# A third FFN chunk by seven products, an even mixing rate, and every fourth plain FFN residual summed by an accumulating DMA

## The chip, the cores and the metric

The kernel runs on one core of one Trainium2 chip, as one program. The metric is the device time of one execution in microseconds; three runs are given, and one further execution was profiled.

## The reference, cut to what matters

Two layers, each a mixer and a SwiGLU feed-forward part (FFN), each followed by a layer norm, on x of 256 tokens by 2048, all in float32. The change lies in the FFN of both layers (D_FF is 5632, eleven chunks of 512):

```python
def swiglu(x, w_gate, w_up, w_down):
    return (jax.nn.silu(x @ w_gate) * (x @ w_up)) @ w_down
...
        y = swiglu(x, ffn_w_gate[layer], ffn_w_up[layer], ffn_w_down[layer])
        x = layer_norm(DEEPNORM_ALPHA * x + y, ln_g[layer, 1], ln_b[layer, 1])
```

## The kernel before, in words

**Precision by halves.** A float32 product is made of three matmuls: every operand w is split into a high half (a rounded copy, `wh`) and a residual (`wl` = w - wh). ScalarE writes the copy (L425) and VectorE the residual (L427). The activations are kept split as XH, XL (input of the FFN) and YH, YL (its gated product).

**Pieces and visits.** A chunk is 512 columns of one weight matrix; its name is its kind, layer and number (g0_2 is gate 2 of layer 0, u is up, d is down). A piece is 256 rows of a chunk (512 KB): gate and up chunks have 8, down chunks 4 or 6. A visit is the work of TensorE on one piece. A plain visit has 12 matmuls of 512 columns (L117 to L119). Gate chunks 2 to 10, and the up chunks in `UPS` (4 and 8), are done instead with seven products for eight, after Strassen: 21 matmuls of 256 columns a visit (L453 to L455). For that VectorE first makes combinations of the weights in the raw buffer (L383, L385, L386), ScalarE copies seven quarters (L389) and VectorE takes their residual (L392). When such a chunk is complete it is drained from its four PSUM banks (`drain_s`, one operation of ScalarE and five of VectorE), and an up chunk drained so is multiplied by the gate on VectorE (L1093). A plain up chunk is multiplied straight from PSUM (L1089, two operations). The combinations of the activations (XS) are made in four batches by `xs_batch` on VectorE and ScalarE (L901 to L914) during up 0.

**The order on TensorE** is written out beforehand in the list `visits`. `ffn_part` lists the plain visits (`flat`: gate 1, the plain ups, the downs of finished groups), and mixes the seven-product visits (`gates`) in: behind plain visit k of `flat` the amount `want` grows by a rate, and as many of them are placed as its whole part says. Behind the ends of odd ups (`near`) at least one is placed. `after_up` fixes the visits behind which the gated product of a chunk is transposed on TensorE (L602, by `h_T`) and split into YH and YL.

**Feeding.** The weights come through SP's queue (L360) into raw buffers: four for plain pieces (N), two for seven-product pieces (S); so too for the split results. In the stretch of a layer in which seven-product visits are mixed in, plain pieces may use N buffers only (`classes`). After every visit `feed_more` issues what loads and splits the free buffers allow, in order of the pieces; a split may run ahead of its visit by as many pieces as there are buffers. The loads are issued in order, and a load whose buffer is not free holds up all behind it. `feed_split` issues a split. For a seven-product piece the copy and the residual are kept back (`owe`), and issued with the next split (`pay`) or one visit later. Each engine works in the order of issue.

Of the kernel before, what the change touches and what calls it, by code (L numbers as in the profile page):

```python
# [9 lines left out]
F32 = mybir.dt.float32  # L10
F32R = mybir.dt.float32r
AF = mybir.ActivationFunctionType
ALU = mybir.AluOpType
# [40 lines left out]
def trunk_kernel(ctx: ExitStack, tc: tile.TileContext, x, ab_w_in, b_f, ab_w_out,  # L54
                 rel_bias, mla_w_in, q_g, kv_g, w_uq, w_ukv, mla_w_out, w_gate, w_up,
                 w_down, ln_g, ln_b, cst, out):
    nc = tc.nc
# [111 lines left out]
    for g in range(4):  # L169
        q0, k0, v0 = ((QA, KA, VA) if g < 2 else (QB, KB, VB))  # L170
        h4 = HB4[g] % 8
        if g == 0:
            c = add_chunk("v0", "X", K16, ([260, 260], lambda h: rows(
                w0, h * 256, [(0, 520, VA + 512)])), ("mm", "att"))
        else:
            c = add_chunk(f"v{g}", "X", K16, ([512], lambda h, a=v0 + h4 * P: rows(
                w0, h * 256, [(0, 512, a)])))
        kmajor(c)
        for u in range(2):
            a = (h4 + 2 * u) * P  # L180
            c = add_chunk(f"qk{g}{u}", "X", K16, ([512], lambda h, a=a, q0=q0, k0=k0: rows(
                w0, h * 256, [(0, 256, q0 + a), (256, 256, k0 + a)])))
# [14 lines left out]

    GROUPS = ((0, 1), (2, 3), (4, 5), (6, 7), (8, 9, 10))
    NF = 11
    UPS = (4, 8)  # L200
    PLAIN = (0, 1)
    h_done = set()
    after_up = {}
# [2 lines left out]
    def ffn_part(layer):  # L206
        def wide(nm, w, f):
            return add_chunk(f"{nm}{layer}_{f}", "X", K16, ([512], lambda h: rows(
                w[layer], h * 256, [(0, 512, f * 512)])))

        def down(gi):
            grp = GROUPS[gi]
            slots = [4 * (f % 4) + k for f in grp for k in range(4)]
            for n in range(4):
                c = add_chunk(f"d{layer}_{gi}_{n}", "Y", slots, (
                    [512], lambda h, n=n: rows(
                        w_down[layer], grp[0] * 512 + h * 256, [(0, 512, n * 512)])))
                if gi == len(GROUPS) - 1 and n == 3:
                    (lead_final if layer == 1 else lead_end)(c)
                else:  # L220
                    kmajor(c)

        g0 = wide("g", w_gate, 0)
        g0.pair = 0
        lead_begin(g0)
        base = len(visits)
        for f in range(NF):
            if f == 1:
                kmajor(wide("g", w_gate, 1))
            c = wide("u", w_up, f)  # L230
            if f in UPS:
                c.S = True
            else:
                kmajor(c)
            if f in (1, 3, 5, 7):
                down(f // 2)
        down(len(GROUPS) - 1)
        flat = visits[base:]
        del visits[base:]
        ends = {}  # L240
        for f in range(NF):
            if f not in UPS:
                e = ends[f] = max(k for k, v in enumerate(flat) if v[0].name == f"u{layer}_{f}")
                o = e + 2 - f % 2
                after_up[layer, f] = [(v[0].name, v[1], v[2]) for v in flat[o:o + 3]]
        gates = []
        for f in range(len(PLAIN), NF):
            c = wide("g", w_gate, f)
            c.S = True
            gates += [(c, h, (0, 1)) for h in range(8)]  # L250
            if f in UPS:
                gates += [(chunks[f"u{layer}_{f}"], h, (0, 1)) for h in range(8)]
        near = {ends[f] + 2 for f in (1, 3, 5, 7, 9)}
        ns, want = 0, 0.0
        for k, v in enumerate(flat):
            visits.append(v)
            want = max(want + (0 if k < 9 else 0.575 if k < 62 else 0.74 if k < 132 else 0.9),
                       ns + 1 if k in near else 0)
            while ns < min(len(gates), int(want)):
                visits.append(gates[ns])  # L260
                ns += 1
                c = gates[ns - 1][0]
                f = int(c.name[3:])
                if ns % 8 == 0 and c.name[0] == "g" and f not in UPS:
                    assert k < ends[f] - 1, (k, ns, ends)
        assert ns == len(gates)
        for f in UPS:
            e = max(k for k, v in enumerate(visits) if v[0].name == f"u{layer}_{f}")
            rest = [v for v in visits[e + 1:] if not v[0].S]
            o = next(k for k, v in enumerate(rest) if v[1] == 0)  # L270
            after_up[layer, f] = [(v[0].name, v[1], v[2]) for v in rest[o:o + 2]]
# [4 lines left out]
    c = add_chunk("m0", "X", K16, ([512], lambda h: rows(wi, h * 256, [(0, 512, 0)])))  # L276
    lead_begin(c)
    for i in (1, 2):
        c = add_chunk(f"m{i}", "X", K16, ([288], lambda h, i=i: rows(
            wi, h * 256, [(0, 288, 512 + 288 * (i - 1))])), ("att",) if i == 1 else None)  # L280
# [4 lines left out]
    for nm in order:  # L285
        p = int(nm[2:])
        if nm[0] == "u":
            c = add_chunk(nm, "X", [0, 1, 2, 3], ([384], lambda h, p=p: rows(
                w_uq[0], h * 256, [(0, 384, p * 384)])))
        else:  # L290
            c = add_chunk(nm, "X", [4, 5, 6, 7], ([512], lambda h, p=p: rows(
                w_ukv[0], h * 256, [(0, 512, p * 512)])))
# [6 lines left out]
    pieces = []  # L299
# [9 lines left out]
    first_s, last_s = {}, {}  # L309
# [4 lines left out]
    raw_free = [("N", feed.tile([P, HPMAX], F32, name=f"raw{i}")) for i in range(NR)]  # L314
# [5 lines left out]
    slot_of, rslot_of = {}, {}  # L320
# [44 lines left out]
    whole = {}  # L365
    owed = []
# [12 lines left out]
    def split_s(j):  # L379
# [14 lines left out]
        wts[j] = (sh.rearrange("p (q c) -> p q c", c=256), sl.rearrange("p (q c) -> p q c", c=256))  # L394
        return hi, lo

    def feed_split(j, halves=False, part=None):
        if j >= len(pieces):
            return False
        c, h = pieces[j]  # L400
        n = 2 * c.n
        if part != 1:
            got = take(w_free, j) if j in raws else None
            if got is None:
                return False
            slot_of[j] = got
            if c.S:
                new = split_s(j)
                for o in owed:
                    o["age"] += 1  # L410
                pay("act")
                pay("dve")
                owe(j, *new)
                return True
            r = raws.pop(j)
            wh, wl = got[1]
            wts[j] = (wh[:, :n].rearrange("p (k c) -> p k c", k=2),
                      wl[:, :n].rearrange("p (k c) -> p k c", k=2))
            whole[j] = (r, wh, wl)
        r, wh, wl = whole[j]  # L420
        cuts = [(0, c.n), (c.n, n)] if halves or part is not None else [(0, n)]
        if part is not None:
            cuts = [cuts[part]]
        for a, b in cuts:
            nc.scalar.activation(wh[:, a:b], r[:, a:b], AF.Copy)  # L425
            pay("act")
            nc.vector.tensor_tensor(wl[:, a:b], r[:, a:b], wh[:, a:b].bitcast(F32),  # L427
                                    op=ALU.subtract)
            pay("dve")
        if part != 0:  # L430
            whole.pop(j)
            raw_free.append(rslot_of.pop(j))
        for o in owed:
            o["age"] += 1
        return True
# [921 lines left out]
    for i, (c, h, toks, *half) in enumerate(visits):  # L1357
# [21 lines left out]
        if last_use[c.name, h] == i:  # L1379
            j = pid[c.name, h]  # L1380
# [81 lines left out]
```

## Time and profile before

| | us |
|---|---|
| median of three runs | 2145.41 |
| lowest and highest | 2145.27, 2146.47 |
| the profiled execution | 2146.55 |
| its span, first to last instruction | 2144.7 |
| TensorE busy in the span | 2120.4 |
| VectorE busy | 1674.0 |
| ScalarE busy | 1061.6 |
| GpSimd busy | 94.5 |

Matmuls are pipelined and the profile models their ends, so a busy TensorE is read by the starts of its instructions. The mixed stretch runs from about 463 to 1052 us in layer 0 and from about 1460 to 2050 in layer 1.

### The profile page before, as it was taken

The page shows a single profiled execution, that of the slowest core. Times are in us where ns is not written, and L with a number is a line of the kernel's source. Part 1 is how long each engine was busy: PE and PEld are TensorE (multiplying, and loading weights), DVE is VectorE, ACT ScalarE, POOL GpSimd, SP SyncE. Part 2 cuts the span into 40 slices and gives each one's busy share as a digit, 9 for nine tenths or more (in the row PEclk, how much of TensorE's full clock was granted, in tenths as well). Part 3 has the DMA queues.
Part 4 walks back from the last instruction along what each step waited for, and adds up shares of the span by engine and source line. Part 5 has one row for each costly group of instructions (what it writes and reads, how often), then busy time and mean ns, then how long its engine had stood idle before and what let it go on. Part 6 is the DMA issues. An engine that isn't in the chain of part 4 may idle for free.

```text
span 2144.7 us, 31708 instructions
## 1 busy us (share of the span) xinstructions
PE 2120.4 (99%) x12570; PEld 1864.7 (87%) x12570; DVE 1674.0 (78%) x2173; ACT 1061.6 (50%) x1212; POOL 94.5 (4%) x142
## 2 busy tenths in 40 slices
PE   9999999999999999999999999999999999999998
PEld 9899998788888888888888999878888888888886
DVE  5555656798888998899866676688888989889875
ACT  5444544355545555555534665445444555555551
POOL 2100000100000000000001331010000000000000
PEclk9999999999999999999999999999999999999999
DMA  8565555556555556555865533745555556555582
GB/s 287 176 204 165 172 184 199 198 174 207 195 191 190 189 190 203 187 187 184 295 193 164 176 129 137 284 139 182 188 189 192 180 190 203 187 190 199 184 293 77
DMA packets 230341, 410.41 MB, mean 191 GB/s; under 512 B 14089, under 2 KB 58161, under 8 KB 229169
## 3 DMA queue, kind: packets, MB, share of 16 engines
q1 hardware_dynamic: 230192, 408.40, 57.3%
q8 instruction: 98, 1.61, 0.3%
q14 instruction: 51, 0.41, 0.1%
HBM read 402.56 MB, written 5.78 MB: 190 GB/s over the span
## 4 chain that ended last, share of the span: by engine, by line
PE 58%; issue 35%; DVE 5%; ACT 1%; POOL 1%; DMA 0%; SPq 0%; DVEq 0%; ACTq 0%; POOLq 0%
PE mm L117 11%; PE mm L118 11%; PE mm L119 11%; PE mm L512 3%; PE mm L516 3%; PE mm L514 3%; PE tp L602 2%; PE att L118 1%; PE att L119 1%; PE att L117 1%; PE sA L454 1%; PE sB L454 1%; PE sC L454 1%; PE sC L455 1%; PE sB L453 1%
## 5 line engine op out<-in xcount | busy, mean ns | idle before, releaser
L425 ACT ACTIVATE wh<-raw 128x1024 fp32r<-128x1024 f32 (+3 forms) x403 | 417.5, 1040 | 416.2 <-PE mm L119 161.9
L427 DVE TENSOR_TENSOR wl<-raw,wh 128x1024 fp32r<-128x1024 f32 (+3 forms) x403 | 482.3, 1206 | 133.1 <-ACT wh L425 131.9
L392 DVE TENSOR_TENSOR sl<-sraw,sh 128x1792 fp32r<-128x1792 f32 x176 | 356.2, 2024 | 64.6 <-ACT sh L389 63.9
L389 ACT ACTIVATE sh<-sraw 128x1792 fp32r<-128x1792 f32 x176 | 298.9, 1698 | 145.1 <-DVE sraw L386 141.9
L117 PE MATMUL mm<-wh,XH 128*128 128x512 f32 (+3 forms) x820 | 319.9, 390 | 0.0
L118 PE MATMUL mm<-wl,XH 128*128 128x512 f32 (+3 forms) x820 | 316.8, 386 | 0.0
L119 PE MATMUL mm<-wh,XL 128*128 128x512 f32 (+3 forms) x820 | 316.3, 386 | 0.0
L117 PE MATMUL mm<-wh,YH 128*128 128x512 f32 (+1 forms) x768 | 303.9, 396 | 0.0
L118 PE MATMUL mm<-wl,YH 128*128 128x512 f32 (+1 forms) x768 | 302.9, 394 | 0.0
L119 PE MATMUL mm<-wh,YL 128*128 128x512 f32 (+1 forms) x768 | 302.4, 394 | 0.0
L119 PEld LDWEIGHTS mm<-wh,XL 128*128 128x128 f32 x820 | 153.9, 188 | 33.2
L117 PEld LDWEIGHTS mm<-wh,XH 128*128 128x128 f32 x820 | 154.4, 188 | 28.0
L118 PEld LDWEIGHTS mm<-wl,XH 128*128 128x128 f32 x820 | 154.1, 188 | 27.7
L119 PEld LDWEIGHTS mm<-wh,YL 128*128 128x128 f32 x768 | 144.1, 188 | 34.6
L117 PEld LDWEIGHTS mm<-wh,YH 128*128 128x128 f32 x768 | 144.5, 188 | 29.6
L118 PEld LDWEIGHTS mm<-wl,YH 128*128 128x128 f32 x768 | 144.2, 188 | 29.5
L383 DVE TENSOR_TENSOR sraw<-sraw 128x512 f32<-128x512 f32 x176 | 120.5, 685 | 0.0
L512 PE MATMUL mm<-XH,wh 128*128 128x256 f32 x364 | 104.3, 286 | 0.0
L514 PE MATMUL mm<-XH,wl 128*128 128x256 f32 x364 | 102.6, 282 | 0.0
L516 PE MATMUL mm<-XL,wh 128*128 128x256 f32 x364 | 102.5, 282 | 0.0
L453 PE MATMUL sA<-sh,XH 128*128 128x256 f32 x352 | 100.9, 287 | 0.0
L454 PE MATMUL sA<-sl,XH 128*128 128x256 f32 x352 | 98.8, 281 | 0.5 <-DVE sl L392 0.4
(302 smaller groups left out, 4447.6 us busy)
## 6 DMA issues: line engine op xcount, KB each, us to landing
raw<-in_ffn_w_down_dram SPq DMA_DIRECT2D x160, 512.0 KB, 5.2
sraw<-in_ffn_w_gate_dram SPq DMA_DIRECT2D x149, 512.0 KB, 3.9
raw<-in_ffn_w_up_dram SPq DMA_DIRECT2D x137, 512.0 KB, 4.7
raw<-in_ab_w_in_dram SPq DMA_DIRECT2D x80, 256.0 KB, 3.1
sraw<-in_ffn_w_up_dram SPq DMA_DIRECT2D x39, 512.0 KB, 3.9
raw<-in_ffn_w_gate_dram SPq DMA_DIRECT2D x27, 512.0 KB, 4.6
sraw<-in_ab_w_in_dram SPq DMA_DIRECT2D x48, 256.0 KB, 3.3
raw<-in_ab_w_out_dram SPq DMA_DIRECT2D x22, 512.0 KB, 3.6
```

The lines of the kernel that those rows point to most:

```text
L117: nc.tensor.matmul(o, lh, rh, start=start, stop=False)
L118: nc.tensor.matmul(o, lh, rl, start=False, stop=False)
L119: nc.tensor.matmul(o, ll, rh, start=False, stop=stop)
L389: nc.scalar.activation(sh, r[:, 256:2048], AF.Copy)
L392: nc.vector.tensor_tensor(sl, r[:, 256:2048], sh.bitcast(F32), op=ALU.subtract)
L425: nc.scalar.activation(wh[:, a:b], r[:, a:b], AF.Copy)
L427: nc.vector.tensor_tensor(wl[:, a:b], r[:, a:b], wh[:, a:b].bitcast(F32), op=ALU.subtract)
L453: nc.tensor.matmul(o, h, w[0][:, q], start=first, stop=False)
L454: nc.tensor.matmul(o, h, w[1][:, q], start=False, stop=False)
L512: nc.tensor.matmul(o, wh[:, kk, a:a + P], XH[:, slot, :], start=first, stop=False)
L514: nc.tensor.matmul(o, wl[:, kk, a:a + P], XH[:, slot, :], start=False, stop=False)
L516: nc.tensor.matmul(o, wh[:, kk, a:a + P], XL[:, slot, :], start=False, stop=last)
```

## The change

Up 2 joins the chunks that are done by seven products, in both layers; so 96 visits a layer are mixed in among 165 (172 in layer 1) plain ones, where it was 88 among 173 (180). The rate at which they are mixed in is 0.77 from plain visit 7 on, where it was 0.575 from visit 9, 0.74 from 62 and 0.9 from 132. And for each fourth plain piece (counted over the whole kernel), if it belongs to an up or a down chunk and lies in the mixed stretch, VectorE no longer takes the residual: ScalarE copies the high half, then writes its negative into wl, and GpSimd issues a DMA that adds the raw weights to wl in SBUF. This branch does not issue what a seven-product piece is owed.

```diff
-    UPS = (4, 8)
+    UPS = (2, 4, 8)
...
-            want = max(want + (0 if k < 9 else 0.575 if k < 62 else 0.74 if k < 132 else 0.9),
+            want = max(want + (0 if k < 7 else 0.77),
                        ns + 1 if k in near else 0)
...
+    nth = {}
+    for j, (c, h) in enumerate(pieces):
+        if not c.S:
+            nth[j] = len(nth)
+
+    def by_dma(j):
+
+        c, h = pieces[j]
+        y = c.name[1]
+        return (c.name[0] in "ud" and y in first_s and first_s[y] + 6 < j < last_s[y]
+                and nth[j] % 4 == 0)
+
     def feed_split(j, halves=False, part=None):
...
+        if part is None and by_dma(j):
+            nc.scalar.activation(wh[:, :n], r[:, :n], AF.Copy)
+            nc.scalar.activation(wl[:, :n], wh[:, :n].bitcast(F32), AF.Copy, scale=-1.0)
+            nc.gpsimd.dma_start(out=wl[:, :n].bitcast(F32), in_=r[:, :n], accum_op=ALU.add)
+            whole.pop(j)
+            raw_free.append(rslot_of.pop(j))
+            for o in owed:
+                o["age"] += 1
+            return True
```

## Rows read from the trace of the kernel before

**Rows 1.** The head of the page: span, and busy time of each engine
```profile
span 2144.7 us, 31708 instructions
...
PE 2120.4 (99%) x12570; PEld 1864.7 (87%) x12570; DVE 1674.0 (78%) x2173; ACT 1061.6 (50%) x1212; POOL 94.5 (4%) x142
```

**Rows 2.** Windows view, mixed stretch of layer 0: PE, PEld, DVE, ACT, POOL, clock, DMA, GB/s
```profile
463.00:1052.00 589.00, 586.49 (x3459) 514.07 (x3458) 522.93 (x601) 304.78 (x259) 0.00 (x0) 1.00 0.58 193
```

**Rows 3.** Timeline of TensorE: start us, us, instruction; first matmuls of three visits
```profile
800.53 0.28 PE L453 MATMUL sA<-sh,XH 128*128 128x256 f32 x1
...
803.00 0.39 PE L117 MATMUL mm<-wh,YH 128*128 128x512 f32 x1
...
805.79 0.28 PE L453 MATMUL sA<-sh,XH 128*128 128x256 f32 x1
```

**Rows 4.** Timeline of TensorE, transposes of the gated product: idle time and its releaser in brackets
```profile
527.41 0.66 PE L602 MATMUL tp<-ident,gt 128*128 128x128 f32 x4 [0.70 <-DVE gt L1089]
...
702.93 0.66 PE L602 MATMUL tp<-ident,gt 128*128 128x128 f32 x4 [1.35 <-DVE gt L1093]
...
1460.19 0.65 PE L602 MATMUL tp<-ident,gt 128*128 128x128 f32 x4 [0.50 <-DVE gt L1089]
...
1524.35 0.33 PE L602 MATMUL tp<-ident,gt 128*128 128x128 f32 x1 [1.30 <-DVE gt L1089]
```

**Rows 5.** Groups by line and shape: count, busy us, mean ns, idle before and its releaser
```profile
L427 DVE TENSOR_TENSOR wl<-raw,wh 128x1024 fp32r<-128x1024 f32 x379 | 459.4, 1221 | 117.2 <-ACT wh L425 116.0
...
L425 ACT ACTIVATE wh<-raw 128x1024 fp32r<-128x1024 f32 x379 | 399.0, 1057 | 408.3 <-PE mm L119 160.7 <-DMA raw<-in_ffn_w_down_dram 83.3 <-DMA raw<-in_ffn_w_up_dram 71.4
...
L392 DVE TENSOR_TENSOR sl<-sraw,sh 128x1792 fp32r<-128x1792 f32 x176 | 356.2, 2024 | 64.6 <-ACT sh L389 63.9
...
L389 ACT ACTIVATE sh<-sraw 128x1792 fp32r<-128x1792 f32 x176 | 298.9, 1698 | 145.1 <-DVE sraw L386 141.9 <-PE mm L119 2.3 <-PE sC L455 0.4
...
L383 DVE TENSOR_TENSOR sraw<-sraw 128x512 f32<-128x512 f32 x176 | 120.5, 685 | 0.0
...
L385 DVE TENSOR_TENSOR sraw<-sraw 128x256 f32<-128x256 f32 x176 | 74.8, 425 | 6.1
...
L489 DVE TENSOR_TENSOR gt<-gt,sC 128x512 f32<-128x512 f32 x18 | 12.4, 687 | 1.9
```

**Rows 6.** Timeline of both layers before the first seven-product visit, VectorE and TensorE
```profile
445.06 1.22 DVE L901 TENSOR_TENSOR xt<-XH,XL 128x1024 f32<-128x1024 f32 x1
...
463.01 1.28 DVE L1089 TENSOR_TENSOR gt<-gt,mm 128x512 f32<-128x512 f32 x2
...
463.88 0.60 PE L602 MATMUL tp<-ident,gt 128*128 128x128 f32 x4
...
1455.45 2.02 DVE L392 TENSOR_TENSOR sl<-sraw,sh 128x1792 fp32r<-128x1792 f32 x1 [0.63 <-ACT sh L389]
...
1458.86 1.28 DVE L1089 TENSOR_TENSOR gt<-gt,mm 128x512 f32<-128x512 f32 x2
```

**Rows 7.** Timeline: first copy of a plain piece, first matmul of its visit (two pieces)
```profile
1904.77 1.99 ACT L425 ACTIVATE wh<-raw 128x1024 fp32r<-128x1024 f32 x2
...
1912.94 0.39 PE L117 MATMUL mm<-wh,XH 128*128 128x512 f32 x1
...
1663.87 1.05 ACT L425 ACTIVATE wh<-raw 128x1024 fp32r<-128x1024 f32 x1
...
1676.99 0.39 PE L117 MATMUL mm<-wh,YH 128*128 128x512 f32 x1
```

**Rows 8.** DMA issues: KB each, median us from issue to landing
```profile
raw<-in_ffn_w_down_dram SPq DMA_DIRECT2D x160, 512.0 KB, 5.2
...
B<-in_ln_b_dram SPq DMA_DIRECT2D x4, 1024.0 KB, 8.8
```

**Rows 9.** Timeline of GpSimd: the same instruction twice
```profile
1238.80 0.46 POOL L1251 TENSOR_TENSOR qt<-qt,COS 128x128 f32<-128x128 f32 x1
...
1240.44 1.53 POOL L1251 TENSOR_TENSOR qt<-qt,COS 128x128 f32<-128x128 f32 x1
```

## The prediction

> **What bounds the kernel now.** I read the head of the page first: TensorE is busy for 2120.4 of 2144.7 us [rows 1]. Ends of matmuls are modelled, so I next read starts. In the timeline of TensorE a plain visit (12 matmuls of 512 columns) runs from 803.00 to 805.79, 2.79 us; a seven-product visit (21 of 256) from 800.53 to 803.00, 2.47 us [rows 3]. Nothing stands between them: in the FFN stretches the kernel is bound by the number of matmul columns. The exceptions there are short waits of TensorE in front of the transposes of the gated product; they end with VectorE's multiplication [rows 4]. Last I read the stretch in which seven-product visits are mixed in: VectorE is busy for 522.9 of 589 us (88.8%), ScalarE for 304.8, GpSimd not at all, the DMA share is 0.58 and the granted clock 1.00 [rows 2]. So VectorE is the engine that must not be asked for more, and the change asks in one place and gives in another.
>
> **Part one: up 2 by seven products.** Eight visits a layer go from 2.79 to 2.47 us: 16 x 0.32 = **-5.1 us** on TensorE's own chain, the only certain term. VectorE pays for it: the combinations and the residual of such a piece take 0.69 + 2 x 0.43 + 2.02 = 3.57 us against 1.22 for a plain one, ScalarE 1.70 against 1.06 [rows 5]. Draining the chunk takes two operations of 0.69, three of half that width (0.43 each, the row with 256 columns), and a multiplication of 1024 columns (1.22, the row of that width), against two of 0.68 for a plain up: 2.5 us more. Together 8 x 2.35 + 2.5 = 21.3 us a layer on VectorE.
>
> **Part two: residuals by DMA.** Counting in the code, 29 pieces a layer fulfil the condition (pieces 0 and 4 of a plain up and piece 0 of a down chunk, from the seventh piece behind the first seven-product one up to the last). Each takes 1.22 us off VectorE [rows 5]: -35.4 us a layer. Net VectorE has 522.9 + 21.3 - 35.4 = 508.8 us to do in a stretch of about 586: 86.8%, a little under now. ScalarE copies twice: 29 x 1.06 + 8 x 0.64 + 0.4 = 36 us more, 341 of 586, 58%. Neither becomes the bound as a mean, so the averages cost nothing; what is hidden here would show if VectorE were asked for some 13% more.
>
> What counts is lateness. Such a piece is now ready after two copies (2.1 us), GpSimd's issue and the transfer. I paired the start of the first copy with the start of the visit for the 87 plain pieces of layer 1 that follow a seven-product piece directly, as most of the 58 do: the shortest lead is 8.17 us (1904.77 to 1912.94), the middle one 13.1 (a piece near it: 1663.87 to 1676.99) [rows 7]. No accumulating transfer stands in the trace. From below, it takes as long as a load of 512 KB, 5.2 us; from above, it reads two operands of 512 KB and so takes as long as the 1 MB loads, 8.8 us [rows 8]. GpSimd's issue I bound by its small operations, 0.46 and 1.53 us [rows 9]. So the piece is ready 7.8 to 12.4 us after its first copy starts. I take 9.1 (2.1 + 1.0 + 6.0), nearer to the load because neither side is HBM. Over the 87 leads the mean shortfall is 0.035 us at 9.1, nothing at 7.8, 0.48 at 11.9 and 0.63 at 12.4. Times 58: **+2 us**, with bounds 0 and +37. It also holds its raw buffer until it lands, and SP, which issues in order, would wait with the next load of that buffer; with four such buffers in rotation I put that at nothing while the transfer is short, and into the upper bound otherwise.
>
> The new branch doesn't pay the owed half of the seven-product piece before it, so that copy starts one copy (1.06 us) later, and may go out a visit later. But the 1.22 us residual that stood before its subtraction on VectorE is gone. The two about cancel: 0.
>
> The Trainium skill (DMA: Bandwidth & Descriptors, section Anatomy of one DMA) gives a transfer issued by GpSimd as about 2.0 us plus its bytes over 436 GB/s. By that 512 KB would be an estimated 3.2 us, the piece would be ready after 6.3, and this term would be 0; the page's fit is for a plain copy with no other traffic, and no row here shows one.
>
> **Part three: the new order.** I wrote out the visits from the two rate lines. Three transposes change their cover. Up 1: a seven-product visit now stands between its end and the transposes, 2.47 us more cover, against waits of 0.70 and 1.30: both go, -2.0. Up 4: two plain visits behind its last product where one stood, so 2.79 us more against 1.35 in layer 0, and layer 1 repeats it: -2.7. Up 2: one plain visit behind its last product, as up 4 now: +1.35 in each layer, +2.7 [rows 4]. Net **-2.0 us**.
>
> The start of the stretch gets worse. The first seven-product visit moves from behind three plain visits of gate 1 to behind one, and up 0's transposes fall behind one such visit instead of none: 2.47 us more cover. But splits are issued by buffers that come free, about four plain pieces ahead, and now two seven-product pieces, not one, are split while VectorE still makes the sums for XS. I listed by the code what is queued in front of up 0's multiplication (L1089). In layer 0 VectorE works from 445.06 to 463.01 almost without a gap, and TensorE's transposes start at 463.88 as soon as the first half is there [rows 6]. Added in front: the first piece's residual (2.02), the whole second piece (3.57) and a plain residual that slides in (1.22), less 0.7 of earlier start and at most 1.2 of gaps that fill: 4.9 to 6.1 us. The multiplication starts at 467.9 to 469.1, its first half ends 0.65 later, the visits reach the transposes at 463.88 + 2.47 = 466.35: a stall of 2.2 to 3.4 us. In layer 1 the first piece's residual (1455.45) stands before the multiplication (1458.86) already [rows 6], and there is a wait of 0.50 [rows 4]; the second piece (3.57) and two plain residuals (2.4) come in front, less up to 1.0 of earlier start: 5.0 to 6.0, less 2.47 of cover, so 2.5 to 3.5 more than now. Behind it queue the splits of the next pieces, but they have TensorE's stall to catch up. Together **+4.7 to +6.9; I take +6**.
>
> **Sum.** -5.1 - 2.0 + 6 + 2 = +0.9 on the profiled execution's 2146.55 us (the span of 2144.7 and 1.85 around it): 2147.4. That execution lay 1.1 above the median of the three runs, so **2146.3 us**. A time within 0.2% of before (2141.1 to 2149.7) is what this measurement can't tell from no change.
>
> **Rivals.**
> *In time and no stall at the start* (faster). If the multiplication of up 0 isn't delayed past its cover, since sums for XS run earlier than I think when VectorE has less before them, and transfers land in time, only -5.1 - 2.0 remain: 2138.3. For it: VectorE's order there hangs on which buffer is free, which I could only list. Against: 88.8% busy as a mean, and no gap in that stretch. It decides when less than 2.5 us is added in front of L1089.
> *The transfer is late* (slower). At 11.9 us the shortfall is 0.48 x 58 = 28 in place of 2: 2146.3 + 26 = 2172; at 11.0 (0.24 x 58 = 14) 2158. For it: the transfer shares its engines with loads that already fill 0.58 of them, and loads of 512 KB take 5.2 us. Against: no HBM side. It decides from an issue to landing of some 8 us.
> *GpSimd is held up by VectorE.* GpSimd's multiplication L1251 takes 0.46 us, and 1.53 beside a busy VectorE [rows 9]. If issuing is held up by an operation of VectorE of up to 2 us on top of the 8.8, ready at 13.6: 1.24 x 58 = 72, so 2216. For it: VectorE is busy 88.8% here. Against: each instruction would have to meet the longest one. The Trainium skill (SBUF — State Buffer, section Who interferes with whom) says that GpSimd's descriptor writing starves while VectorE holds the shared port pair in its two-port modes, and that an operation of two tensors has none; most operations in this stretch are of two tensors, so by that page this rival is weak.
>
> **How the numbers follow.** Forecast (no change that can be told) 0.36; in time and no stall 0.26; transfer late 0.31; held up 0.07. Faster 0.26, same 0.36, slower 0.38. The range leaves out the held-up case, what of the late case goes beyond 11.9 us, and the lowest few per cent of the fast one: **2138 to 2172**. The forecast's own range is 2141 to 2150.
>
> **What the changed profile would show.** Seven-product visits of up 2 of 2.47 us, 192 in all. VectorE near 87% and ScalarE near 58% in the stretch. TensorE's wait for L1089 at the start of each stretch 2 to 4 us; none behind up 1 and up 4, 1.3 us behind up 2. Matmuls that wait for a DMA into wl: a few, under 1 us each. I am wrong if the accumulating transfers take over 8 us (then waits of one to several us at every fourth plain piece), if seven-product matmuls wait for sl in numbers, or if the start shows no wait.

## The result, and the profile after

The changed kernel took 2226.9 us (median of four runs, 2221.8 to 2230.7) beside 2145.9 for the kernel before on the same chip (2145.3 to 2146.8): a ratio of 1.0375, 95% interval 1.0354 to 1.0397, or +80.9 us. It is slower, far outside the range of 2138 to 2172, and beyond the slowest rival's 2216 too.

The page of the changed kernel: its head, the queue that GpSimd fills, groups, DMA issues. Its line numbers stand 21 higher from `feed_split` on (L602 is now L623, L932 L953, L1089 L1110, L1093 L1114).

```profile
span 2225.6 us, 32199 instructions
...
PE 2145.8 (96%) x12714; PEld 1886.8 (85%) x12714; DVE 1649.8 (74%) x2171; ACT 1133.0 (51%) x1272; POOL 145.0 (7%) x200
...
q0 software_dynamic: 8352, 30.41, 7.1%
...
L392 DVE TENSOR_TENSOR sl<-sraw,sh 128x1792 fp32r<-128x1792 f32 x192 | 388.7, 2024 | 133.8 <-ACT sh L389 132.9
...
L475 PE MATMUL sA<-sl,XH 128*128 128x256 f32 x384 | 111.4, 290 | 23.0 <-DVE sl L392 22.9
L436 POOL DMA_DIRECT2D wl<-raw x58 | 50.5, 871 | 1247.2 <-ACT wl L435 1012.7
...
wl<-raw POOLq DMA_DIRECT2D x58, 512.0 KB, 5.3
```

The windows view of its two mixed stretches (us from to; length, then PE, PEld, DVE, ACT, POOL; granted clock, DMA share, GB/s):

```profile
463.00:1094.00 631.00, 602.20 (x3559) 527.42 (x3558) 514.88 (x604) 343.06 (x293) 25.33 (x29) 0.99 0.67 207
1495.00:2134.00 639.00, 605.21 (x3561) 530.29 (x3560) 515.68 (x605) 342.24 (x293) 25.17 (x29) 0.98 0.67 207
```

Against [rows 1, 2] the engines' work is as forecast: VectorE 514.9 us in the stretch (508.8 forecast), ScalarE 343.1 (341), and the transfer lands after 5.3 us in the median (6.0 taken). Only the stretch is longer: 631 us where 586 was expected. VectorE, the engine that was to be spared, is now busy for 82% of it, and waits: 133.8 us in front of the seven-product residual (L392), where it was 64.6 [rows 5], both nearly all for ScalarE's copy. TensorE, which before stood still in these stretches almost only at transposes, waits for that residual 23.0 us.

The timeline of TensorE in layer 0, in order of time: the transposes that wait (up 0, up 2, up 4 and, further down, up 8; the row of up 2 shows three of its four), between the last two a matmul that waits for an accumulating transfer, and at the end a late seven-product visit:

```profile
471.04 0.66 PE L623 MATMUL tp<-ident,gt 128*128 128x128 f32 x4 [2.71 <-DVE gt L1110]
...
569.34 0.90 PE L623 MATMUL tp<-ident,gt 128*128 128x128 f32 x3 [2.71 <-DVE gt L1114]
...
729.80 1.11 PE L623 MATMUL tp<-ident,gt 128*128 128x128 f32 x4 [2.49 <-DVE X L953]
...
848.73 0.50 PE L118 MATMUL mm<-wl,YH 128*128 128x512 f32 x1 [1.44 <-DMA wl<-raw]
...
997.41 0.66 PE L623 MATMUL tp<-ident,gt 128*128 128x128 f32 x4 [3.44 <-DVE X L953]
...
1051.57 0.38 PE L474 MATMUL sA<-sh,XH 128*128 128x256 f32 x1
1053.63 0.40 PE L475 MATMUL sA<-sl,XH 128*128 128x256 f32 x1 [1.68 <-DVE sl L392]
...
1057.04 0.40 PE L476 MATMUL sC<-sh,XS 128*128 128x256 f32 x1
1057.25 0.30 PE L474 MATMUL sC<-sh,XH 128*128 128x256 f32 x1
1057.39 0.28 PE L475 MATMUL sC<-sl,XH 128*128 128x256 f32 x1
1057.51 0.28 PE L476 MATMUL sC<-sh,XL 128*128 128x256 f32 x1
```

In [rows 4] the longest such wait was 1.35 us. The last six rows show a second price. After the wait that follows the matmul at 1051.57 the matmuls of 256 columns follow each other at 0.21 us instead of 0.118, until 1057.25. The windows view ahead of it, in it and behind it:

```profile
1047.60:1051.60 4.00, 3.97 (x23) 3.09 (x21) 1.27 (x2) 3.97 (x5) 0.87 (x1) 1.00 0.25 50
1053.60:1057.10 3.50, 3.46 (x17) 3.47 (x18) 2.76 (x5) 1.70 (x1) 0.00 (x0) 0.54 0.70 216
1058.00:1062.00 4.00, 4.00 (x19) 3.24 (x18) 3.52 (x5) 2.43 (x2) 0.00 (x0) 1.00 0.46 139
```

The granted clock is 0.54 there, the lower of the two levels (1.2 GHz), behind a wait of 1.94 us (two starts 2.06 us apart where 0.118 is usual; the profile models the end of the first matmul later and shows 1.68 us of it as idle). 17 matmuls at 0.21 cost 1.6 us more than at 0.118. Not each wait is followed by it: of the 19 waits of 1.9 us or more, counted so, in the two FFN parts of the changed kernel 11 are (granted clock of the next 4 us 0.50 to 0.69), and of the six between 1.4 and 1.75 us none. The FFN of the kernel before has no wait that long, and its clock stays at 1.00.

### Where TensorE's time goes

For this table every gap between the starts of two TensorE matmuls in the two FFN parts was taken, less the usual spacing (0.233 us for 512 columns, 0.118 for 256, 0.109 for a transpose), and put down to the releaser that the timeline names: us in both layers. "Stretched" sums the surpluses of 0.04 to 0.25 us; in the changed kernel some two thirds of it fall where the granted clock is at the lower level, in the kernel before none. The variants are those of the experiments below; "against before" is the median against that of the kernel before on the same chip.

| | before | e9 | e13 | e10 | e4 | e1 | e15 | e16 | after |
|---|---|---|---|---|---|---|---|---|---|
| transposes, for the gated product | 6.0 | 6.0 | 8.0 | 8.0 | 8.0 | 9.9 | 9.6 | 10.8 | 10.8 |
| transposes, for residual additions (X) | 1.4 | 1.4 | 0.7 | 3.3 | 2.4 | 11.5 | 12.3 | 14.5 | 15.7 |
| seven-product visits, for sl | 0.8 | 1.2 | 7.4 | 2.6 | 7.2 | 4.0 | 8.1 | 16.7 | 26.9 |
| the same, for sh or a drained bank | 0 | 0 | 1.1 | 3.7 | 1.0 | 0 | 0.4 | 5.7 | 4.4 |
| plain matmuls, for wl's transfer | 0 | 0 | 0 | 0.6 | 0 | 0 | 0 | 0 | 7.4 |
| plain matmuls, for YH or YL | 0 | 0 | 0.9 | 0 | 0.7 | 7.1 | 4.4 | 5.2 | 4.2 |
| stretched | 4.7 | 4.5 | 8.6 | 9.4 | 8.5 | 16.8 | 13.6 | 18.3 | 23.6 |
| **against before** | | +0.2 | +13.1 | +15.7 | +15.9 | +30.8 | +31.6 | +55.3 | +80.9 |

The column "after" less the column "before" is +80.1; some 3.4 us of smaller waits come to it, and -5.1 of fewer matmul columns go off: 78 of the 81 us.

### The profile page after: what moved, and what is told of

The parts are those of the page before. It is cut to its first block, busy times and chain, and to the rows that moved or that the text cites. A ratio compares the mean times of both kernels' runs of the same rounds, so it can differ in the third digit from the quotient of the medians.

```text
span 2225.6 us, 32199 instructions
## 1 busy us (share of the span) xinstructions
PE 2145.8 (96%) x12714; PEld 1886.8 (85%) x12714; DVE 1649.8 (74%) x2171; ACT 1133.0 (51%) x1272; POOL 145.0 (7%) x200
## 3 DMA queue, kind: packets, MB, share of 16 engines
q1 hardware_dynamic: 230192, 408.40, 55.3%
## 5 line engine op out<-in xcount | busy, mean ns | idle before, releaser
L446 ACT ACTIVATE wh<-raw 128x1024 fp32r<-128x1024 f32 (+4 forms) x335 | 347.2, 1040 | 350.8 <-DMA raw<-in_ffn_w_down_dram 119.4
L448 DVE TENSOR_TENSOR wl<-raw,wh 128x1024 fp32r<-128x1024 f32 (+4 forms) x335 | 401.9, 1205 | 152.3 <-ACT wh L446 149.8
L392 DVE TENSOR_TENSOR sl<-sraw,sh 128x1792 fp32r<-128x1792 f32 x192 | 388.7, 2024 | 133.8 <-ACT sh L389 132.9
L389 ACT ACTIVATE sh<-sraw 128x1792 fp32r<-128x1792 f32 x192 | 326.0, 1698 | 192.3 <-DVE sraw L386 132.9
L118 PE MATMUL mm<-wl,XH 128*128 128x512 f32 (+3 forms) x768 | 297.8, 388 | 3.6 <-DMA wl<-raw 3.6
L117 PE MATMUL mm<-wh,XH 128*128 128x512 f32 (+3 forms) x768 | 300.1, 391 | 0.0
L119 PE MATMUL mm<-wh,XL 128*128 128x512 f32 (+3 forms) x768 | 296.8, 386 | 0.0
L119 PEld LDWEIGHTS mm<-wh,XL 128*128 128x128 f32 x768 | 145.2, 189 | 30.7
L475 PE MATMUL sA<-sl,XH 128*128 128x256 f32 x384 | 111.4, 290 | 23.0 <-DVE sl L392 22.9
L436 POOL DMA_DIRECT2D wl<-raw x58 | 50.5, 871 | 1247.2 <-ACT wl L435 1012.7
L474 PE MATMUL sB<-sh,XS 128*128 128x256 f32 x384 | 109.6, 285 | 0.0
L475 PE MATMUL sB<-sl,XS 128*128 128x256 f32 x384 | 109.5, 285 | 0.0
```

The lines of the kernel that those rows point to most:

```text
L117: nc.tensor.matmul(o, lh, rh, start=start, stop=False)
L118: nc.tensor.matmul(o, lh, rl, start=False, stop=False)
L119: nc.tensor.matmul(o, ll, rh, start=False, stop=stop)
L389: nc.scalar.activation(sh, r[:, 256:2048], AF.Copy)
L392: nc.vector.tensor_tensor(sl, r[:, 256:2048], sh.bitcast(F32), op=ALU.subtract)
L436: nc.gpsimd.dma_start(out=wl[:, :n].bitcast(F32), in_=r[:, :n], accum_op=ALU.add)
```

## The experiments

**The two parts apart, and the payment.** e1 switches the branch off; e2 puts the branch alone into the kernel before (31 pieces a layer meet its condition there, 29 in the new order); e3 and e4 let it issue what a seven-product piece is owed.

```diff
 e1: -        if part is None and by_dma(j):
     +        if False and part is None and by_dma(j):
 e2:  the function by_dma and the branch, put into the kernel before
 e3, e4 (in the branch of the changed kernel, and of e2), behind dma_start:
     +            pay("act")
     +            pay("dve")
```

> The changed kernel with the new branch switched off: up 2 by seven products and the rate of 0.77, every residual on VectorE. Theory O (the order costs: seven-product pieces come too closely for VectorE's chain, the DMA only helps): at least as slow as the changed kernel, 60 to 120 us above before, with waits of seven-product matmuls for sl of over 27 us. Theory B (the new branch costs: two copies on ScalarE in front of a seven-product piece whose halves it does not issue): -5.1 of matmuls, -2.0 of covers and about +4 at the start, so -4 to +10 us against before, waits for sl under 8 us.

> The kernel before with the new branch alone: the old chunks and rates, every fourth plain up or down piece in the mixed stretch (31 a layer) summed by DMA. Theory O: VectorE has 38 us a layer less to do and the order is the old one, so -4 to +8 us against before. Theory B: most of the loss is here, +40 to +80 us, with the waits for sl and for the residual additions that the changed kernel shows.

> The changed kernel, and the branch issues what a seven-product piece is owed behind its DMA, as the plain branch does. Theory B in the form that the order of issue costs: most of the loss goes, 0 to +25 us against before. In the form that the two copies in front on ScalarE cost (1.06 us a piece): little changes, +60 to +85. Theory O: little changes, +60 to +85.

> The kernel before with the branch that issues what is owed. Theory B, order of issue: within 8 us of before. Theory B, two copies: as the kernel with the branch alone. Theory O: within 8 us of before, as the kernel with the branch alone.

Measured: e1 2177.5 us, ratio 1.0137 [1.0121, 1.0154], +30.8; e2 2165.2, 1.0086 [1.0071, 1.0101], +18.5; e3 2218.9, 1.0333 [1.0307, 1.036], +72.2; e4 2162.7, 1.0077 [1.0062, 1.0092], +15.9. Both parts cost by themselves, and together they cost 81 where the sum is 49. e1 and e2 fall between what the two theories gave for them, so neither theory holds alone. The missing payment accounts for some 9 us in the changed kernel (e3's interval is +66 to +77, that of the changed kernel +76 to +85, so the 9 are barely clear of noise) and for 2.6 in the old order, which the intervals don't tell from nothing: at most a part of it, not the cause.

**What of the branch costs: old order.** Six variants of the branch in the order of the kernel before, each without some of its steps. Without the second copy or the transfer the low half of these pieces is incomplete; of these variants only the time is read.

```diff
 e5: the branch of e2 without dma_start
 e6: the branch of e2 without the second copy (L435)
 e9:  wh copy; pay("act"); pay("dve")                    (nothing else)
 e14: wh copy                                            (nothing else)
 e13: wh copy; second copy; pay("act"); pay("dve")       (no transfer)
 e10: wh copy; dma_start; pay("act"); pay("dve")         (no second copy)
```

> The kernel before with the new branch, but without its DMA: wl stays the negative copy, the adding of the raw weights is left out. Theory S (the second copy on ScalarE delays the seven-product piece behind it): the whole loss of the branch alone stays, +14 to +20 us against before. Theory D (the transfer costs: its traffic, its late landing, the raw buffer that it holds): the loss goes, -2 to +6.

> The kernel before with the new branch, but without its second copy: the raw weights are added to what lay in wl, the negative copy is left out. Theory S: the loss goes, -2 to +6 us against before. Theory D: it stays, +14 to +20. If both lie in between, both parts carry some of it.

> The branch of the change in the old order, reduced to its saving: the plain pieces it takes (31 in each layer) get ScalarE's first copy and pay what is owed of a seven-product piece, and nothing else; VectorE's residual, ScalarE's second copy and the accumulating transfer are all left out, so the low half of these pieces is not computed. Theory A (each of the branch's additions delays the next seven-product piece or a transposed chunk by itself, and any one of them is enough): with none of them nothing is late, 2140 to 2147 us, and TensorE's waits for the low half of the seven-product weights stay near the 0.8 us of the kernel before. Theory B (the time is lost by what is removed: without VectorE's residual in its place the work that follows moves up and takes VectorE in a worse order): 2158 us or more again, as in the four variants of the branch so far.

> The branch in the old order with ScalarE's first copy alone: no residual, no second copy, no transfer, and nothing paid (the low half of these pieces is left out). Theory A (payment is worth little: e2 against e4 differed by 2.6 us, e6 against e10 by 0): 2145 to 2150 us. Rival (a seven-product piece that is left owed for one more piece is late by itself): 2155 to 2162 us.

> The branch in the old order with both of ScalarE's copies and the payment, but no accumulating transfer (adding the raw weights to the negative copy is left out, so the low half of these pieces is wrong). Theory A (the second copy, 1.06 us on ScalarE ahead of the high half that is owed, makes the low half of the next seven-product piece late whether it is paid here or not): 2157 to 2162 us, with TensorE's waits for the low half near 7 us as in e5. Rival (the 14.4 us of e5 came from the payment that it left out): 2145 to 2149 us, as in e9.

> The branch in the old order with the accumulating transfer and with the payment of what is owed, but without ScalarE's second copy (the negative copy of the high half is left out, so the low half is wrong by it). The variant with the transfer and without payment took 15.7 us more than the kernel before. Theory A (the second copy delays the high half of the next seven-product piece, the missing payment delays its low half and bunches VectorE's work; the transfer is free): 2142 to 2150 us. Rival (the transfer itself costs, through the software queue's issue and its share of the DMA engines): 2155 to 2163 us, with TensorE waiting for transfers or for the transposed chunks.

| variant | us | ratio, 95% interval |
|---|---|---|
| e5, both copies, no transfer, no payment | 2160.9 | 1.0065 [1.005, 1.008] |
| e6, one copy, transfer, no payment | 2162.3 | 1.007 [1.0055, 1.0085] |
| e9, one copy, no transfer, payment | 2146.2 | 1.0 [0.999, 1.001] |
| e14, one copy, no transfer, no payment | 2146.3 | 1.0 [0.9991, 1.0009] |
| e13, both copies, no transfer, payment | 2159.8 | 1.0064 [1.0049, 1.0079] |
| e10, one copy, transfer, payment | 2161.8 | 1.0071 [1.0056, 1.0086] |

In e10 the expectation of theory A (the transfer is free) failed, and its rival held. e5 and e6, which leave out one step each, cost nearly as much as e2 (18.5), so no one step was the cause; e9, e14, e13 and e10 settle it: in this order the payment costs nothing, the second copy alone 13 us, the transfer alone 16, and both together no more than one of them (e4, 15.9). One thing more differs in e10: without the second copy the transfer doesn't wait for it. GpSimd issues it 0.1 us after the start of the first copy in the median (0.6 in e16 below), and 2.56 us after it in e4 and in the changed kernel. So e10 prices a transfer that starts over 2 us earlier than that of the branch. And the saving itself is worth nothing. The windows view of e9 for the stretch of [rows 2], and its group for L392:

```profile
463.00:1052.00 589.00, 586.20 (x3457) 513.82 (x3456) 486.09 (x570) 303.92 (x259) 0.00 (x0) 1.00 0.59 194
...
L392 DVE TENSOR_TENSOR sl<-sraw,sh 128x1792 fp32r<-128x1792 f32 x176 | 356.1, 2023 | 124.4 <-ACT sh L389 124.1
```

36.8 us of VectorE's work are gone from this stretch (522.9 before), and over both layers VectorE waits 124.4 us instead of 64.6 in front of L392 for ScalarE. What was taken off VectorE became idle time there, since the copy in front of it comes no sooner.

*How the second copy costs.* Two timelines of ScalarE and VectorE around the same seven-product piece (the last gate activation, L1106 and L1084, is the same operation), first e13:

```profile
859.86 1.06 ACT L1106 ACTIVATE gt<-gt 128x1024 f32<-128x1024 f32 x1 [4.28 <-DVE gt L511]
860.83 1.04 ACT L447 ACTIVATE wh<-raw 128x1024 fp32r<-128x1024 f32 x1
861.77 1.04 ACT L434 ACTIVATE wh<-raw 128x1024 fp32r<-128x1024 f32 x1
862.85 1.06 ACT L435 ACTIVATE wl<-wh 128x1024 fp32r<-128x1024 f32 x1
863.81 1.68 ACT L389 ACTIVATE sh<-sraw 128x1792 fp32r<-128x1792 f32 x1
...
865.53 2.03 DVE L392 TENSOR_TENSOR sl<-sraw,sh 128x1792 fp32r<-128x1792 f32 x1 [2.40 <-ACT sh L389]
...
867.61 0.58 PE L476 MATMUL sA<-sl,XH 128*128 128x256 f32 x1 [1.67 <-DVE sl L392]
```

and the kernel before:

```profile
855.10 1.06 ACT L1084 ACTIVATE gt<-gt 128x1024 f32<-128x1024 f32 x1 [2.79 <-DVE gt L489]
856.07 1.99 ACT L425 ACTIVATE wh<-raw 128x1024 fp32r<-128x1024 f32 x2
857.96 1.69 ACT L389 ACTIVATE sh<-sraw 128x1792 fp32r<-128x1792 f32 x1
...
859.69 2.03 DVE L392 TENSOR_TENSOR sl<-sraw,sh 128x1792 fp32r<-128x1792 f32 x1 [0.18 <-ACT sh L389]
```

From the start of the activation to that of the seven-product copy it is 2.86 us before and 3.95 in e13: 1.09 more, the length of the second copy (1.06). VectorE, which had a residual to do in that time, stands idle for 2.40 us, and the visit waits 0.56 for sh and 1.67 for sl. ScalarE's 58% as a mean says nothing of this: here it has five operations in a row. This is the longest such delay in layer 0; layer 1 has one of the same kind (1.94 us for sl behind 1869.72). The other waits of e13 are shorter and were not followed one by one.

*How the transfer costs.* In e10 the load of the next down piece, issued at 688.64, meets an accumulating transfer that GpSimd issues at 688.04. DMA issues of e10, one issue each: the load, and another load of an up piece at 1999.4, beside the transfer issued at 1997.9:

```profile
raw<-in_ffn_w_down_dram SPq DMA_DIRECT2D x1, 512.0 KB, 7.6
...
raw<-in_ffn_w_up_dram SPq DMA_DIRECT2D x1, 512.0 KB, 8.2
```

and the same two loads in the kernel before, issued at 686.80 and 1987.45:

```profile
raw<-in_ffn_w_down_dram SPq DMA_DIRECT2D x1, 512.0 KB, 4.8
...
raw<-in_ffn_w_up_dram SPq DMA_DIRECT2D x1, 512.0 KB, 4.5
```

The first of them is awaited by ScalarE, and through it by VectorE; in e10 the timeline reads:

```profile
688.04 0.87 POOL L435 DMA_DIRECT2D wl<-raw  x1 [19.19 <-DMA raw<-in_ffn_w_down_dram]
...
696.34 1.06 ACT L447 ACTIVATE wh<-raw 128x1024 fp32r<-128x1024 f32 x1 [3.50 <-DMA raw<-in_ffn_w_down_dram]
...
697.43 1.23 DVE L449 TENSOR_TENSOR wl<-raw,wh 128x1024 fp32r<-128x1024 f32 x1 [1.01 <-ACT wh L447]
...
704.45 1.23 DVE L1115 TENSOR_TENSOR gt<-gt,xt 128x1024 f32<-128x1024 f32 x1
...
705.73 1.11 PE L624 MATMUL tp<-ident,gt 128*128 128x128 f32 x4 [2.32 <-DVE gt L1115]
```

The transposes of up 4 wait 2.32 us where they waited 1.35 [rows 4], behind a chain that starts with the late load. That load was issued no later than before (both kernels' times differ by 1.8 us there); elsewhere in e10 SP does wait for a transfer that holds a raw buffer, nine times and 15.5 us in all, which delays the loads behind. The price of the traffic itself is seen by taking the plain FFN loads singly and pairing each with the same load of the variant that differs by the transfer alone. The 124 loads that are under way beside a transfer in e10 take 5.73 us to land in the mean, and 5.29 in e9; the other 162 take 5.25 and 5.31. In the new order (e16 and e15 below) it is 6.25 and 5.30 for 109 loads, and 5.16 and 5.17 for the other 161. So the transfer is mostly in time itself (waits for it are 0.6 us in e10), and makes the loads beside it late. That these late loads are the whole of the 16 us isn't shown: one wait was followed to its load, and the hold of the raw buffers was not run apart from the traffic.

The Trainium skill (DMA: Bandwidth & Descriptors, section Issuing engines are not separate DMA queues) says that DMAs issued from several engines run on the same set of DMA engines and interleave; these runs agree, with 0.4 to 1.0 us a load. The Trainium skill's fit (the same page, section Anatomy of one DMA) would give the transfer an estimated 3.2 us; measured it is 5.3 in the median of the changed kernel, so here the measurement decides. The prediction took the fit for one of a plain copy with no other traffic; the Trainium skill gives it per DMA there and names neither condition.

**Another place for the payment.** e11 is e2 with the owed copy between ScalarE's two, so that the second copy isn't ahead of it.

```diff
 wh copy
+            pay("act")
 second copy; dma_start
+            pay("dve")
```

> The whole branch in the old order, computing everything, with the high half of the owed seven-product piece paid between ScalarE's two copies and its low half on VectorE right after, so that neither waits for the second copy. Theory A (the +16 us of the branch with payment came from the second copy ahead of the owed high half): TensorE's waits for the low half fall from 7.2 us to about 1, and the time to 2146 to 2153 us. Rival (the second copy costs wherever it stands, or the delay lies elsewhere): 2158 to 2164 us as before.

Measured: 2162.8 us, 1.0074 [1.0059, 1.0089], +16.7; waits for sl 7.7 us. The rival held. The transfer is in this variant too, and its loads beside a transfer are the slowest of all in the old order (6.24 us in the mean, 115 loads), so this run doesn't part the second copy's place from the transfer.

**The order.** e7 is e1, and e8 the kernel before, with the transposes and residual additions of a finished seven-product up chunk one plain visit later.

```diff
-            after_up[layer, f] = [(v[0].name, v[1], v[2]) for v in rest[o:o + 2]]
+            after_up[layer, f] = [(v[0].name, v[1], v[2]) for v in rest[o + 1:o + 3]]
```

> The new order alone (no residual by DMA), and the transposes of the up chunks done by seven products stand one plain visit later. If the wait that I had expected to go (up 4) and to come (up 2) is a matter of cover: the waits for the residual additions (12.0 us in the order alone) and behind up 2 (4.4) fall by at least two thirds, with the slow spacing that follows them, so 10 to 16 us less than the order alone: +15 to +21 against before. If VectorE is late by more than a visit there, under 6 us less.

> The kernel before with the transposes of up 4 and up 8 one plain visit later. In before TensorE waits there for 1.52, 1.51, 0.39 and 0.98 us. If the cover suffices: 3 to 4.4 us less than before. If the later visits wait for YH and YL instead: no change.

Measured: e7 2163.8 us, 1.008 [1.0065, 1.0095], +17.3, 13.5 less than e1's +30.8: the waits for residual additions fall from 11.5 to 0, those for the gated product from 9.9 to 5.5, while those for sl rise from 4.0 to 13.1. e8 2145.1 us, 0.9993 [0.9983, 1.0002]: 1.4 us below the kernel before, which this measurement doesn't tell from nothing. It is the best version that the runs found; none beats the kernel before beyond doubt.

**The branch in the new order.** e15 and e16 are the changed kernel with the steps of e9 and e10; e12 is the changed kernel with those of e11 and e7.

> The changed kernel with its new order, in which the 29 pieces per layer that take the branch have VectorE's residual removed and the owed piece paid, with neither second copy nor transfer (the low half of these pieces is left out). Theory A (the order's cost is VectorE's load, and the branch's saving relieves it; what the branch costs is the transfer and the second copy): 2160 to 2172 us, below the 2177.5 us of the order alone. Rival (the order costs by itself, through visits that come too close for any load of VectorE): 2175 to 2185 us, no gain from the removed work. A result at 2200 us or more would put the excess on the removal.

> The changed kernel with its new order, the accumulating transfer and the payment, without ScalarE's second copy (the negative copy is left out, so the low half of these pieces is wrong by it). Theory A (the transfer delays the loads beside it; in the old order it cost 15.7 us, and loads of weights that overlapped it landed 0.4 to 1.0 us later on average; in the new order less slack is left and it costs more): 20 to 40 us above the run without transfer. Rival (the excess in the new order is the second copy's): within 16 us of the run without transfer, and 20 us or more below the 2218.9 us of the variant with both copies.

> The changed kernel with two edits: the owed high half paid between ScalarE's two copies and the low half after them, and the transposes and residual additions of a finished up chunk one plain visit later. Theory A (the order's cost is late chunks on VectorE, +31 of which the later place took back 14; the branch's cost is late seven-product pieces, which the payment between the copies takes back; the more than additive rest came from both meeting): about 2165 to 2175 us, against 2226.9 for the changed kernel. Rival (the even rate alone makes the two meet, as 0.77 seven-product visits to each plain one in the place of 0.575 at first leave no slack, wherever the copies stand): 2195 to 2215 us.

Measured: e15 2178.3 us, 1.0147 [1.013, 1.0164], +31.6; e16 2202.0, 1.0258 [1.0243, 1.0274], +55.3; e12 2216.9, 1.0327 [1.0312, 1.0343], +70.9. In e15 the rival held: with 58 residuals less to do, the order costs as much as alone (30.8). So the 81 us go in steps: the order 31, the saving 0, the transfer 24 (e15 to e16, in which theory A held; as in e10 it starts earlier than that of the branch), the second copy on top of it 17 (to e3's 72.2), the missing payment 9. By their intervals the last three steps are known to some 5 to 7 us each. On top of the transfer the second copy adds nothing in the old order (e10 to e4) and 17 us here. The second copy without the transfer wasn't run in the new order, so it isn't shown whether the two still hide behind one another in part, and steps taken in another order could share the 50 us of the branch out otherwise. e12 was expected at 2165 to 2175 and missed by 42 us; it lies 2 us above the range of its rival, 2195 to 2215. The later place removes the waits for residual additions here too (15.7 to 0), but those for sl (30.7) and for the transfers (9.6) take their place, and the stretched spacing stays at some 24; what e7 gained in the order alone isn't to be had with the branch.

Why less work doesn't help the order is seen at up 4 of layer 1 in e15, in VectorE's timeline and in TensorE's:

```profile
1728.16 0.69 DVE L510 TENSOR_TENSOR xt<-xt,sC 128x512 f32<-128x512 f32 x1
1728.89 1.23 DVE L1114 TENSOR_TENSOR gt<-gt,xt 128x1024 f32<-128x1024 f32 x1
1730.03 0.68 DVE L383 TENSOR_TENSOR sraw<-sraw 128x512 f32<-128x512 f32 x1
1730.75 0.42 DVE L385 TENSOR_TENSOR sraw<-sraw 128x256 f32<-128x256 f32 x1
1731.21 0.43 DVE L386 TENSOR_TENSOR sraw<-sraw 128x256 f32<-128x256 f32 x1
1731.55 1.22 DVE L448 TENSOR_TENSOR wl<-raw,wh 128x1024 fp32r<-128x1024 f32 x1
1732.68 1.28 DVE L953 TENSOR_TENSOR X<-X,mm 128x512 f32<-128x512 f32 x2
...
1734.02 1.12 PE L623 MATMUL tp<-ident,gt 128*128 128x128 f32 x4 [4.19 <-DVE X L953]
```

The gated product is complete at 1730.1, and the last matmul of TensorE before the wait has run out at 1729.7. But the transposes need the PSUM banks of the down chunk that ended just before them, and its residual additions (L953) are queued behind the five operations of the drain (the last of them is shown), the multiplication, three combinations and a residual: they end at 1734.0. It is a queue of ten operations at one moment, not a mean load, and the pieces that the branch takes don't lie in it.

## Why the prediction was wrong, point by point

- **What bounds the kernel** was read rightly, and one sentence too far: "Neither becomes the bound as a mean, so the averages cost nothing". VectorE's work in the stretch came out 6 us from the forecast, ScalarE's 2. But a busy share of 82 or 87% isn't a reserve when each seven-product piece passes from VectorE to ScalarE and back in a fixed queue. e9 and e15 show it: VectorE's work in the stretch fell by 7 and 6% (e9 against before, e15 against e1), and the time didn't move.
- **Second copy and missing payment, "The two about cancel: 0"**: this step failed. I weighed a later copy against a missing residual on VectorE; but the residual saved is worth 0 (e9), and the copy costs 13 us by itself in the old order (e13) and some 17 on top of the transfer in the new one. In the changed kernel the waits for sl are 26.9 us against 0.8, the largest single item; they are not the second copy's alone: 4.0 with the order alone (e1), 8.1 in e15, 16.7 with the transfer (e16), 22.9 with the second copy as well (e3).
- **The transfer, +2** (bounds 0 and +37): its length was right in the middle, 5.3 us against 6.0 and 0.87 for the issue against 1.0, and the piece was ready 7.8 us after the start of its first copy in the median (7.0 to 13.1) where 9.1 was taken. Ten of the 58 transfers took over 8 us, and waits for them cost 7.4 us. What the step left out is the traffic on the loads beside it. I had looked only at the raw buffer that it holds, and in the changed kernel SP shows no wait for that. The transfer's price, 16 us in the old order and 24 in the new one, is more than waits for it explain; loads beside it land 0.4 and 1.0 us later (e10, e16), and one of the waits behind such a load was followed above.
- **The new order as a whole, -5.1 - 2.0 + 6 = -1.1**: this failed too, by 32 us: e1, which has the order alone, is 30.8 us slower. The next points say where.
- **Cover of the transposes, -2.0**: up 1's waits went, as said. Up 2 waits 2.71 and 2.27 us instead of 1.35. Up 4 was to lose its waits; up 4 and up 8 together wait 15.1 us for the residual additions (2.49, 3.44, 4.88, 4.25), 11.3 more than they waited before (1.35, 0.22, 1.34, 0.81). I counted the visits behind the last product, and not which down chunk ends there and what is queued ahead of its additions on VectorE. e7 shows that the place decides: one visit later, these waits are 0.
- **The start, +6**: 2.71 and 2.47 us were measured against forecasts of 2.2 to 3.4 in layer 0 and 2.5 to 3.5 more in layer 1: right in layer 0, a little high in layer 1 (2.0 more).
- **Not in the sum at all**: the clock. Behind more than half of the waits of 1.9 us or more TensorE runs at the lower level, at up to 1.6 us each. "Stretched" grows by 18.9 us.
- **-5.1 for the columns** wasn't measured apart, but no row speaks against it; with up 1's waits, some 2 us, it is the only gain.
- **The rivals**: the slower side was in them, but for another reason. *The transfer is late* decides from 8 us to landing; the median is 5.3, and ten of 58 are over 8. *GpSimd is held up by VectorE*: its issues take 0.87 us in the mean and 1.09 at most, and VectorE's operations are no slower (L392 2024 ns in both kernels). *In time and no stall at the start*: the stall is there.

What stays open: e1's 31 us are located (additions, half clock, waits for YH and YL), and the later transposes take back 13.5 of them, but up 2 and the even rate weren't run apart. Nor was it tried in what place the second copy would be free, nor what it costs in the new order without the transfer, nor what a transfer costs alone that starts as late as that of the branch.

## What to carry to other kernels

Work taken off an engine with a high mean load was worth nothing here (e9, e15); look first whether the trace shows something waiting for that work; before it is moved, follow the chain that it stands in, and price what it becomes on the next engine at the moment when that one has a queue. A transfer that is in time can still cost: ask which loads land at that moment and who waits for them. When an order is changed, list for each point where TensorE needs something (transposes, bank reuse) what is queued ahead of it in the in-order engine, rather than the visits that cover it.

## What the hardware showed that was not expected

- Behind a wait of 1.94 us (from the matmul at 1051.57) TensorE's granted clock stood at 0.54 for 3.5 us; behind another of 1.94 (852.20) and one of 3.61 (993.57) it stayed at 1.00. So the length of a wait alone doesn't tell whether it is paid a second time; none of 1.75 us or less was, in either kernel's FFN.
- An accumulating DMA of 512 KB from SBUF to SBUF, issued by GpSimd, took 5.3 us to land in the median (4.5 to 10.6), about as long as a load of 512 KB (5.2 in the kernel before), and 0.87 us of GpSimd's time. Loads under way beside it landed 0.4 us (e10) to 1.0 us (e16) later than the same loads without it.
- The second copy and the transfer cost 13 and 16 us when each stands alone in the old order, and 16 together there; in the new order the transfer costs 24, and the second copy on top of it 17.
